# Pooled tokens' block sums at other steps and in another order, and the last pooling product copied to SBUF before its gate

## The chip, the cores and the metric

The kernel runs on one core of a Trainium2 chip. The metric is the device time of one execution in microseconds. The engines are TensorE (PE, matmuls), VectorE (DVE), ScalarE (ACT), GpSimd (POOL) and SyncE (SP, which here only issues DMAs). Each works through its own instructions in order and waits for others by semaphores.

## The reference

One encoder layer, float32, 1024 tokens of width 1024:

```python
h = rmsnorm(x, g_mix)
z = h @ w_in                               # pooled 512 | q 1024 | k 1024 | v 1024
y_pool = pool_mixer(z[..., :512], w_pool_grp, pool_scale)
y_attn = diff_attention(q, k, v, ...)      # 8 heads, two softmax maps per head
gates = sigmoid(h @ w_gate + b_gate)       # 2 x 1024 columns
merged = gates[..., :1024] * (y_pool @ w_branch_pool) \
       + gates[..., 1024:] * (y_attn @ w_branch_attn)
x = x + merged @ w_out
h2 = rmsnorm(x, g_ffn)
x = x + square(relu(h2 @ w_up)) @ w_down
```

The change touches how `y_pool @ w_branch_pool` and its gating are carried out.

## The kernel before, in words

Float32 precision is kept by splitting each operand into a high part (a cast to fp32r on ACT, L137) and a low part (the rest, a subtraction on DVE or POOL, L138). Each product is then three matmuls: high by high (L144), high by low (L145) and low by high (L146). A weight is loaded raw by DMA, cast, and subtracted, before PE may use it; its raw tile is free again after the subtraction. There are two raw tiles in a pool named `raw`.

The kernel has two large parts. In the first, up to about 700 us, a loop over steps `g` (from -2 up to some 10 past the 64 attention steps) builds the projection z of each head (weights `wqkv`, raw `rqkv`), the scores, the softmax and the attention's sums; the gate products `g` (weights `fwgate`, raw `frgate`) and other weight preparation are spread over the steps by tables of step numbers. Then come the two branch projections, each as a Strassen-like scheme of seven products in place of eight: block sums of weights and tokens are made ahead, then products "1", "2", "6", "5", "7", "3", "4" in this order go to PSUM banks named X, Y, Z in turn (pX, pY, pZ for the pooling branch; bX, bY, bZ for the attention branch), and their sums are gated. After this come the output projection and the MLP.

The Tile framework's scheduler sets the final order of the instructions on every engine, from the order of the code, the tiles' dependences and its own timeline. So a change of a step number moves instructions on several engines.

The block sums of the pooling branch are made by `pool_item` (L993). An item (n, e, c) loads a [128, 4, 256] tile by two DMAs (L1004), yields, makes four additions or subtractions of 128x256 on POOL (`sub` is L383, `add` L380), and stores the tile by one DMA to `pw_sum` (weights, n = "w") or `py_sum` (tokens, n = "y") at L1021. The index e picks a depth pair (rows e and e + 2 of the source's four blocks) and c a half of the columns. The "w" items take raw tiles at steps 9, 13, 17 and 21 (`PW_AT`); the "y" items take one of two single tiles, tagged "fu" and "mx", at the steps of `PY_AT`, and read `p_dram`, which holds the pooled tokens. The same two tiles are used by other work: "fu" and "mx" hold weight pieces earlier, the mixer's tiles, the tiles yr2 and yb2 of `y_pair` (L388, attention rows and their factors, L400 and L404), and later the gates `gp`. A load into such a tile waits until the last use of what was in it. In the loop (L1056 to L1063) an item is begun at its step, and its second half, the POOL work and the store, runs one step later.

The pooling products are `p_product` calls from L1243 on. Of the last one, "4", each of four results stays in its bank X[i] until `gated` (L1233) multiplies it there by its gates: a `gp` tile loaded from `g_dram` (L1164) and put through a sigmoid on ACT (L1165); the multiply is L1236, on DVE, into the half-rows `mp` in SBUF. The first attention product then needs the same banks, from the pool `pb` of five: it uses weights `wa` (raw `ra`) and tokens `by`.

Of the kernel before, what the change touches and what calls it, by code (L numbers as in the profile page):

```python
# [17 lines left out]
P = 128  # L18
# [31 lines left out]
G_FIRST, G_Z = 9, 13  # L50
F_FROM, F_PACE, F_UNITS = 4, 0.5, 34
PW_AT = [9, 13, 17, 21]
PY_AT = {63: 'fu', 64: 'mx', 66: 'fu', 67: 'mx'}
SUM_AT = [39, 47, 49, 51, 53, 55, 59, 61]
DIG_AT = {6: 'fu', 8: 'mx', 10: 'fu', 12: 'mx', 14: 'fu', 16: 'mx', 18: 'fu', 20: 'mx'}
DIG_AT.update({g: 'r' for g in (11, 15, 19, 23, 31, 33, 35, 37)})
# [13 lines left out]
def encoder_kernel(  # L70
# [21 lines left out]
    nc = tc.nc  # L92
# [36 lines left out]
    def raw(shape, name):  # L129
        return rpool.tile(shape, F32, tag="raw", name=name)  # L130
# [4 lines left out]
    def split(hi, lo, src, lo_eng=None):  # L135

        made = nc.scalar.copy(hi, src)  # L137
        (lo_eng or nc.vector).tensor_tensor(lo, src, f(hi), op=ALU.subtract)  # L138
        return made
# [17 lines left out]
    def w_tile(shape, name, i, dt=F32R):  # L157
        return wpool.tile(shape, dt, tag=f"W{int(i)}", name=name, bufs=N_W // 2)
# [220 lines left out]
    def add(eng, out_, a, b):  # L379
        eng.tensor_tensor(out_, a, b, op=ALU.add)  # L380

    def sub(eng, out_, a, b):
        eng.tensor_tensor(out_, a, b, op=ALU.subtract)  # L383
# [41 lines left out]
    with ExitStack() as ph:  # L425
# [12 lines left out]
        @contextmanager  # L438
        def behind():
            with ExitStack() as stack:  # L440
                for ins in queued.values():
                    stack.enter_context(tc.issue_after(ins))
                yield
# [17 lines left out]
        def load_x(t):  # L461
            xs[t] = htile([P, D], F32, f"x{t}", 1) if t < 2 else ut([P, D], F32, f"x{t}")
            for c in range(0, D, 512 if t < 2 else D):
                e = c + 512 if t < 2 else D
                loads[f"x{t}"] = q(nc.sync.dma_start, xs[t][:, c:e], x[t * P : (t + 1) * P, c:e])
# [20 lines left out]
        def norm_x(t):  # L486
            if t % 4 == 0:
                hT.update(alloc_T(htile, "hT", t // 4))
            norm_transpose(xs.pop(t), gmb, t, hT, hn_tile(t), sp, [(ps_t, "tr"), (ps_s, "sc")])
# [165 lines left out]
        def distances():  # L655

            di = ut([P, S], I32, "di")
            nc.gpsimd.iota(di, pattern=[[-1, S]], base=S - P, channel_multiplier=1)
            nc.scalar.activation(dist, di, AF.Abs)
            nc.gpsimd.memset(dist[0:64, S - 64 : S], MASKED)  # L660

        def columns():
            cols_ps = ps_t.tile([P, 512], F32, tag="tr", name="cols_ps")
            nc.tensor.transpose(cols_ps[:, 0:32], rows, identf[0:32, 0:32])
            nc.vector.tensor_copy(cols, cols_ps[:, 0:32])
            nc.tensor.transpose(cols_ps[:, P : 2 * P], gg2.rearrange("p a b -> p (a b)"), identf)
            nc.vector.tensor_copy(gcol, cols_ps[:, P : P + 1])
            nc.vector.tensor_scalar(gs, cols[:, 20:21], 1.0 - LAMBDA_INIT, None, op0=ALU.mult)
# [324 lines left out]
        def pool_item(n, e, c, room):  # L993

            name = f"p{n}{e}{c}"
            if room == "r":
                t = raw([P, 4, 256], name)
            else:
                t = fq.tile([P, S], F32, tag=room, name=name).rearrange("p (b c) -> p b c", b=4)
            src, dst = (w_branch_pool, pw_sum) if n == "w" else (p_dram, py_sum)  # L1000
            cs = slice(c * 256, (c + 1) * 256)
            for i in range(2):
                d = e + 2 * i
                nc.sync.dma_start(  # L1004
                    t[:, 2 * i : 2 * i + 2, :],
                    src[d * P : (d + 1) * P, :].rearrange("p (j c) -> p j c", j=2)[:, :, cs],
                )
            yield
            b11, b12, b21, b22 = (t[:, i, :] for i in range(4))
            eng = nc.gpsimd  # L1010
            if n == "w":
                add(eng, b22, b12, b22)
                sub(eng, b12, b11, b12)
                sub(eng, b11, b22, b11)
                sub(eng, b21, b21, b11)
            else:
                sub(eng, b11, b12, b11)
                sub(eng, b12, b22, b12)
                sub(eng, b22, b22, b11)
                sub(eng, b21, b21, b22)  # L1020
            nc.sync.dma_start(dst[:, e, :, cs], t)  # L1021
            yield

        pool_gens = {}
        pool_items = {"w": [(e, c) for c in range(2) for e in range(2)], "y": [(e, c) for c in range(2) for e in range(2)]}
        dig_gens = {}
        sums = [("o", d, c) for d in range(4) for c in range(2)]
        digs = [(e, c) for e in range(4) for c in range(4)]
# [1 line left out]
        for g in range(-2, N + 10):  # L1030
            for t in range(4, NT):
                if LX[t] == g:
                    load_x(t)
            for t in range(1, NT):
                if NX[t] == g:
                    with tc.issue_after(h_hi[t - 2].ins) if t < 6 else nullcontext():
                        norm_x(t)
            if g == G_DIST:
                with behind():
                    distances()  # L1040
            if g == G_COLS:
                columns()
            for a, gen in dig_gens.items():
                if 0 < g - a < 4:
                    next(gen)
            if g in DIG_AT:
                dig_gens[g] = weight_digits(*digs.pop(0), DIG_AT[g])
                with tc.issue_after(loads["x7"].ins), tc.issue_after(loads["fw"].ins):
                    next(dig_gens[g])
            if g in SUM_AT:  # L1050
                sum_gen = weight_sums(*sums.pop(0))
                next(sum_gen)
            if g - 1 in SUM_AT:
                with tc.issue_after(powered[0].ins):
                    next(sum_gen)
            for n, at in (("w", PW_AT), ("y", PY_AT)):  # L1056
                if g - 1 in at:
                    with tc.issue_after(powered[0].ins) if g < N else nullcontext():
                        next(pool_gens[n])
                if g in at:  # L1060
                    pool_gens[n] = pool_item(n, *pool_items[n].pop(0), "r" if n == "w" else PY_AT[g])
                    with tc.issue_after(loads["x7"].ins), tc.issue_after(loads["fw"].ins):
                        next(pool_gens[n])  # L1063
            if g in Y_AT:
                y_gens[g] = y_pair(*Y_AT[g])
                next(y_gens[g])
            for n in (1, 2):
                if g - n in Y_AT:
                    with tc.issue_after(scored[0].ins):
                        next(y_gens[g - n])  # L1070
            gens = {}
            for tok in ORDER:
                if tok not in gens:
                    i = g - tok[1]
                    gens[tok] = stage(tok[0], i) if 0 <= i < N else iter(())
                next(gens[tok], None)
            for gen in gens.values():
                for _ in gen:
                    pass
            while made < F_UNITS and made < (g - F_FROM) * F_PACE:  # L1080
                next(units)
                made += 1
# [34 lines left out]
    def half(d, th):  # L1117
        return mp[d][:, th * 512 : (th + 1) * 512]
# [8 lines left out]
    def p_block(src, i, j):  # L1127
        return src[2 * i * P : (2 * i + 2) * P, j * 512 : (j + 1) * 512].rearrange("(k p) c -> p k c", p=P)

    def wp_set(j):  # L1130
        rw = raw([P, 2, 512], f"rpw{j}")
        with tc.issue_after(loads['fw'].ins) if j in '5734' else nullcontext():
            nc.sync.dma_start(rw, p_block(w_branch_pool, *PW[j]) if j in PW else pw_sum[:, :, PW_SUM[j], :])
        wp_[j] = []
        for k in range(2):
            w = w_tile([P, 2, 512], f"wp{j}_{k}", B_ORDER.index(j) % 2 == 0)
            with tc.issue_after(exped[0].ins) if j in '26' else nullcontext():
                split(w[:, 0], w[:, 1], rw[:, k, :], nc.gpsimd if j in "126" else dve)
            wp_[j].append(w)
# [93 lines left out]
    def gated(d, th, src):  # L1233
        if d % 2 == 0:
            pg[th] = pool_gates(d, th)
        nc.vector.tensor_tensor(half(d, th), src, pg[th][:, d % 2, :], op=ALU.mult)  # L1236
# [4 lines left out]
    X = [pb.tile([P, 512], F32, tag="b", name=f"pX{i}") for i in range(4)]  # L1241
# [37 lines left out]
        gated(i, 1, half(i, 1))  # L1279
    for i in range(4):  # L1280
        p_product(X[i], "4", i)
        gated(i + 4, 0, X[i])
    wa_set("2")
    by_set("2")
    X = [pb.tile([P, 512], F32, tag="b", name=f"bX{i}") for i in range(4)]
# [69 lines left out]
    y = {}  # L1355
# [95 lines left out]
    X = [o_bank(f"oX{t}", t) for t in range(4)]  # L1451
# [453 lines left out]
```

## Time and profile before

| what | value |
| --- | --- |
| median of 3 runs | 1520.74 us (1519.24 to 1521.63) |
| the profiled execution, own time | 1518.36 us |
| its span in the profile | 1516.4 us |
| PE busy | 1503.7 us, 7566 matmuls |
| DVE, ACT, POOL busy | 1076.3, 819.9, 375.2 us |
| DMA moved | 259.39 MB |

Rows of a timeline give the start in us, the duration (of a row with xN, of all N), the engine, the kernel's line, the operation and its tiles as output<-input; a bracket at the end is the idle time before it and what ended it. L12 is line 12 of the kernel. In a table of waits the three numbers are the total, the count and the longest. In a table of windows, each row gives a stretch, its length, the busy time and count of PE, its weight loads, DVE, ACT and POOL, the granted TensorE clock (1.00 is full), the DMA engines' share and GB/s.

### The profile page before, as it was taken

The page shows a single profiled execution, that of the slowest core. Times are in us where ns is not written, and L with a number is a line of the kernel's source. Part 1 is how long each engine was busy: PE and PEld are TensorE (multiplying, and loading weights), DVE is VectorE, ACT ScalarE, POOL GpSimd, SP SyncE. Part 2 cuts the span into 40 slices and gives each one's busy share as a digit, 9 for nine tenths or more (in the row PEclk, how much of TensorE's full clock was granted, in tenths as well). Part 3 has the DMA queues.
Part 4 walks back from the last instruction along what each step waited for, and adds up shares of the span by engine and source line. Part 5 has one row for each costly group of instructions (what it writes and reads, how often), then busy time and mean ns, then how long its engine had stood idle before and what let it go on. Part 6 is the DMA issues. An engine that isn't in the chain of part 4 may idle for free.

```text
span 1516.4 us, 22163 instructions
## 1 busy us (share of the span) xinstructions
PE 1503.7 (99%) x7566; PEld 1303.8 (86%) x7566; DVE 1076.3 (71%) x2196; ACT 819.9 (54%) x1695; POOL 375.2 (25%) x487
## 2 busy tenths in 40 slices
PE   9999999999999999999999999999999999999999
PEld 8999998999999999888788888888888888888887
DVE  7776768887888777745669899676656687556672
ACT  7656565655556564645554478466555634333331
POOL 4556654353526453630240010000000000000000
PEclk9999999999999999999999999999999999999999
DMA  7234443422434344559976734454433799437750
GB/s 228 74 112 144 133 126 105 127 85 70 144 117 146 98 140 142 175 161 295 330 268 204 236 132 136 156 195 153 153 126 111 284 350 392 160 125 261 226 193 28
DMA packets 221931, 259.39 MB, mean 171 GB/s; under 512 B 13462, under 2 KB 152699, under 8 KB 221819
## 3 DMA queue, kind: packets, MB, share of 16 engines
q1 hardware_dynamic: 204250, 230.55, 46.1%
q10 hardware_dynamic: 17568, 27.44, 5.0%
q8 instruction: 59, 0.97, 0.3%
q14 instruction: 54, 0.43, 0.1%
HBM read 180.31 MB, written 77.63 MB: 170 GB/s over the span
## 4 chain that ended last, share of the span: by engine, by line
PE 92%; DMA 4%; POOL 1%; DVE 1%; ACT 1%; issue 1%; SPq 0%; DVEq 0%; POOLq 0%
PE z L146 6%; PE z L144 6%; PE z L145 6%; PE Da L145 4%; PE Da L146 4%; PE Da L144 4%; PE g L146 4%; PE g L144 4%; PE g L145 3%; PE X L144 3%; PE X L146 3%; PE Db L145 3%; PE Db L146 3%; PE X L145 3%; PE Db L144 3%; PE sc L787 2%
## 5 line engine op out<-in xcount | busy, mean ns | idle before, releaser
L146 PE MATMUL z<-wqkv,hT 128*128 128x384 f32 x512 | 174.0, 340 | 0.3 <-DVE hT L449 0.3
L144 PE MATMUL z<-wqkv,hT 128*128 128x384 f32 x512 | 173.6, 340 | 0.1
L145 PE MATMUL z<-wqkv,hT 128*128 128x384 f32 x512 | 172.9, 338 | 0.0
L798 ACT ACTIVATE s<-s,nm 128x256 f32<-128x256 f32 (+7 forms) x128 | 99.4, 777 | 79.4 <-DVE nm L790 79.1
L720 POOL TENSOR_TENSOR ms<-ms,mhalf 128x4 f32<-128x4 f32 x64 | 71.0, 1110 | 155.4 <-DVE ms L719 147.3
L146 PE MATMUL g<-hT,fwgate 128*128 128x512 f32 x256 | 100.9, 396 | 2.7 <-POOL fwgate L138 2.7
L144 PE MATMUL g<-hT,fwgate 128*128 128x512 f32 x256 | 102.0, 398 | 0.3 <-ACT go L353 0.2
L145 PE MATMUL g<-hT,fwgate 128*128 128x512 f32 x256 | 101.3, 396 | 0.0
L144 PEld LDWEIGHTS z<-wqkv,hT 128*128 128x128 f32 x512 | 96.3, 188 | 2.8 <-ACT hT L449 0.4
L145 PEld LDWEIGHTS z<-wqkv,hT 128*128 128x128 f32 x512 | 96.3, 188 | 2.5 <-DVE wqkv L449 0.3
L146 PEld LDWEIGHTS z<-wqkv,hT 128*128 128x128 f32 x512 | 96.2, 188 | 2.6 <-DVE hT L449 0.8
L790 DVE CUSTOM_DVE_ANT_0 s<-sc,dist 128x512 f32<-128x512 f32 (+3 forms) x128 | 71.8, 568 | 19.4 <-PE sc L788 13.9
L138 DVE TENSOR_TENSOR AS<-s,AS 128x512 fp32r<-128x512 f32 x64 | 43.5, 688 | 34.5 <-ACT AS L137 34.3
L787 PE MATMUL sc<-K,Q 128*128 128x512 f32 (+2 forms) x192 | 66.5, 351 | 0.2 <-DVE nm L790 0.2
L788 PE MATMUL sc<-K,Q 128*128 128x512 f32 (+2 forms) x192 | 65.0, 344 | 0.0
L138 POOL TENSOR_TENSOR wqkv<-rqkv,wqkv 128x384 fp32r<-128x384 f32 x56 | 58.8, 1068 | 21.1 <-ACT wqkv L137 21.0
L146 PEld LDWEIGHTS g<-hT,fwgate 128*128 128x128 f32 x256 | 48.5, 189 | 12.4 <-POOL fwgate L138 3.1
L144 PEld LDWEIGHTS g<-hT,fwgate 128*128 128x128 f32 x256 | 48.4, 189 | 9.1 <-ACT yps L344 0.5
L145 PEld LDWEIGHTS g<-hT,fwgate 128*128 128x128 f32 x256 | 48.5, 190 | 8.6 <-issue 0.2
L138 DVE TENSOR_TENSOR AT_0l<-ta,AT_0h 128x512 fp32r<-128x512 f32 (+1 forms) x48 | 32.0, 666 | 29.9 <-ACT AT_0h L137 26.1
L383 POOL TENSOR_TENSOR wd<-wd 128x128 f32<-128x128 f32 (+1 forms) x64 | 49.8, 783 | 8.2 <-ACT wd L985 5.6
L138 POOL TENSOR_TENSOR fwgate<-frgate,fwgate 128x512 fp32r<-128x512 f32 x32 | 42.5, 1333 | 37.0 <-ACT fwgate L137 36.8
(536 smaller groups left out, 4658.2 us busy)
## 6 DMA issues: line engine op xcount, KB each, us to landing
wd<-in_w_down_dram SPq DMA_DIRECT2D x48, 512.0 KB, 6.4
wu<-in_w_up_dram SPq DMA_DIRECT2D x32, 512.0 KB, 5.0
udS<-us SPq DMA_DIRECT2D x64, 256.0 KB, 3.9
ur<-udS SPq DMA_DIRECT2D x32, 512.0 KB, 4.0
rqkv<-in_w_in_dram SPq DMA_DIRECT2D x64, 192.0 KB, 3.0
ur<-ud SPq DMA_DIRECT2D x24, 512.0 KB, 4.0
frgate<-in_w_gate_dram SPq DMA_DIRECT2D x32, 256.0 KB, 2.6
g_dram<-go ACTq DMA_DIRECT2D x32, 256.0 KB, 2.3
```

What stands on the lines that cost most here:

```text
L138: (lo_eng or nc.vector).tensor_tensor(lo, src, f(hi), op=ALU.subtract)
L144: nc.tensor.matmul(ps, lhs_hi, rhs_hi, start=first, stop=False, **kw)
L145: nc.tensor.matmul(ps, lhs_hi, rhs_lo, start=False, stop=False, **kw)
L146: return nc.tensor.matmul(ps, lhs_lo, rhs_hi, start=False, stop=last, **kw)
L383: eng.tensor_tensor(out_, a, b, op=ALU.subtract)
L720: powered[0] = nc.gpsimd.tensor_tensor(ms, ms, mhalf[:, 0:4], op=ALU.pow)
L787: nc.tensor.matmul(dst, Q[:, i, 0, :], rhs, start=True, stop=False)
L788: nc.tensor.matmul(dst, Q[:, i, 1, :], rhs, start=False, stop=True)
L790: nc.vector.tensor_tensor_reduce(out=s[i][:, c : c + w], in0=sc[:, 0:w], in1=dist[:, o0 + c : o0 + c + w], scale=2.0 ** -(h + 1), scalar=B ...
L798: exped[0] = nc.scalar.activation(s[i][:, 0:n], s[i][:, 0:n], AF.Exp, bias=last, scale=-1.0, accum_out=Z[:, i, t : t + 1])
```

## The change

Four edits, and one of spelling.

The "y" items begin at steps 50, 52, 63 and 64; before, at 63, 64, 66 and 67. They are taken by depth pair, both column halves of e = 0 first, then both of e = 1; before, both e of the first column half came first.

The second half of an item runs two steps after its load; before, one. For that the generators are kept under (n, step), since two may be open at a time. This holds for the "w" items too.

The last pooling product is copied by ACT from its bank to its half-row `mp`, and the gating multiply reads and writes that half-row.

```diff
-PY_AT = {63: 'fu', 64: 'mx', 66: 'fu', 67: 'mx'}
+PY_AT = {50: 'fu', 52: 'mx', 63: 'fu', 64: 'mx'}
...
-        pool_items = {"w": [(e, c) for c in range(2) for e in range(2)], "y": [(e, c) for c in range(2) for e in range(2)]}
+        pool_items = {"w": [(e, c) for c in range(2) for e in range(2)], "y": [(e, c) for e in range(2) for c in range(2)]}
...
             for n, at in (("w", PW_AT), ("y", PY_AT)):
-                if g - 1 in at:
+                if g - 2 in at:
                     with tc.issue_after(powered[0].ins) if g < N else nullcontext():
-                        next(pool_gens[n])
+                        next(pool_gens[n, g - 2])
                 if g in at:
-                    pool_gens[n] = pool_item(n, *pool_items[n].pop(0), "r" if n == "w" else PY_AT[g])
+                    pool_gens[n, g] = pool_item(n, *pool_items[n].pop(0), "r" if n == "w" else PY_AT[g])
                     with tc.issue_after(loads["x7"].ins), tc.issue_after(loads["fw"].ins):
-                        next(pool_gens[n])
+                        next(pool_gens[n, g])
...
     for i in range(4):
         p_product(X[i], "4", i)
-        gated(i + 4, 0, X[i])
+        nc.scalar.copy(half(i + 4, 0), X[i])
+        gated(i + 4, 0, half(i + 4, 0))
```

In the compiled order, the four item loads of the changed kernel read the tiles py00, py01, py10 and py11 in this order; before, py00, py10, py01 and py11.

More of the change, by code (lines that the diff above doesn't have):

```diff
@@ L1130, in wp_set @@
     def wp_set(j):
-        rw = raw([P, 2, 512], f"rpw{j}")
+        rw = raw([P, 2, 512], f'rpw{j}')
         with tc.issue_after(loads['fw'].ins) if j in '5734' else nullcontext():
```

## The prediction

> **What bounds the kernel now.** I read the page's busy times first, then its chain, then TensorE's waits, and last the stretches around the two largest of these.
>
> ```profile
> span 1516.4 us, 22163 instructions
> PE 1503.7 (99%) x7566; PEld 1303.8 (86%) x7566; DVE 1076.3 (71%) x2196; ACT 819.9 (54%) x1695; POOL 375.2 (25%) x487
> PE 92%; DMA 4%; POOL 1%; DVE 1%; ACT 1%; issue 1%; SPq 0%; DVEq 0%; POOLq 0%
> ```
>
> TensorE (PE) is busy for 99% of the span and is 92% of the chain. The change takes no matmul away, so all that it can win is time in which PE waits or runs at a lower clock. The view of PE's waits lists these, longest first (microseconds in total, times, longest):
>
> ```profile
> PE g L146 <- POOL fwgate L138: 2.7, 1, 2.7
> ...
> PE bY L144 <- ACT wa L137: 0.9, 1, 0.9
> ...
> PE bX L144 <- DVE mp L380: 0.8, 1, 0.8
> PE bX L146 <- POOL wa L138: 0.6, 1, 0.6
> ```
>
> One wait stands out, a gate product for a weight's low part; the next ones, save two, are in the attention branch's products bX and bY. Both places have windows of their own. The columns after the length are busy time and count for PE, PEld, DVE, ACT and POOL, the granted clock, the DMA share and GB/s:
>
> ```profile
> 641.26:648.69 7.43, 4.71 (x14) 3.36 (x13) 3.92 (x6) 1.95 (x5) 4.13 (x5) 0.77 0.95 299
> 738.86:775.56 36.70, 34.22 (x145) 26.75 (x145) 19.59 (x30) 19.38 (x31) 15.01 (x10) 1.00 0.84 301
> ```
>
> The pitch of an undisturbed 128x512 product is read where bX ends and bZ begins; the first and the last row are five products apart, so 1.13 / 5 = 0.227 us:
>
> ```profile
> 774.43 0.39 PE L145 MATMUL bX<-by,wa 128*128 128x512 f32 x1
> ...
> 775.56 0.39 PE L144 MATMUL bZ<-by,wa 128*128 128x512 f32 x1
> ```
>
> **Stall A, 641 to 649 us.** PE's timeline, then POOL's, with ACT's cast of the weight (the number in brackets is the wait before the row):
>
> ```profile
> 641.26 0.39 PE L145 MATMUL g<-hT,fwgate 128*128 128x512 f32 x1
> 644.36 0.55 PE L146 MATMUL g<-hT,fwgate 128*128 128x512 f32 x1 [2.72 <-POOL fwgate L138]
> 645.13 0.63 PE L145 MATMUL g<-hT,fwgate 128*128 128x512 f32 x1
> 645.56 0.63 PE L146 MATMUL g<-hT,fwgate 128*128 128x512 f32 x1
> 648.69 0.39 PE L144 MATMUL g<-hT,fwgate 128*128 128x512 f32 x1
> ```
> ```profile
> 636.75 0.60 ACT L137 CAST fwgate<-frgate 128x512 fp32r<-128x512 f32 x1
> ```
> ```profile
> 635.60 0.74 POOL L383 TENSOR_TENSOR py<-py 128x256 f32<-128x256 f32 x1 [6.29 <-DMA py<-p_dram]
> ...
> 640.04 3.05 POOL L383 TENSOR_TENSOR py<-py 128x256 f32<-128x256 f32 x4
> 643.05 2.50 POOL L138 TENSOR_TENSOR fwgate<-frgate,fwgate 128x512 fp32r<-128x512 f32 x2
> ```
>
> The cast was done at 637.35, but POOL works in order, and the eight `py` subtractions of two pooled items hold it until 643.05. PE issues nothing from 641.26 to 644.36; then its pitch is 645.56 - 645.13 = 0.43 us until 648.69. The window holds 14 matmuls, 13 of them 128x512: 13 x 0.227 and some 0.07 for the 128x128 one is 3.0 us of work, so the stall costs 7.43 - 3.0 = **4.4 us**, 2.9 as a gap and 1.5 as a lower clock (0.77 granted over the window).
>
> A rule of the Trainium skill bears on that split: "TensorE: Matmul & The Clock Gate", Part 1 (The HAM clock gate), lets the clock fall after an idle window of about 3.4 us. By it a gap this long would not lower the clock and A would be worth 2.9; the rows show a lowered clock after 2.72 us of idling, and the measurement decides.
>
> **Stall B, 738 to 776 us.** The last pooling product's four banks (pX) are read by the gating multiply straight from PSUM, and that waits for the gates (`gp`, a load and a sigmoid). PE's timeline, then DVE's and ACT's:
>
> ```profile
> 738.63 0.39 PE L146 MATMUL pX<-py,wp 128*128 128x512 f32 x1
> 739.80 0.47 PE L144 MATMUL bX<-by,wa 128*128 128x512 f32 x1 [0.78 <-DVE mp L380]
> 742.70 0.50 PE L146 MATMUL bX<-by,wa 128*128 128x512 f32 x1 [0.63 <-POOL wa L138]
> 751.11 0.50 PE L144 MATMUL bY<-by,wa 128*128 128x512 f32 x1 [0.88 <-ACT wa L137]
> 752.98 0.50 PE L146 MATMUL bY<-by,wa 128*128 128x512 f32 x1 [0.19 <-POOL wa L138]
> ```
> ```profile
> 750.48 1.29 DVE L1236 TENSOR_TENSOR mp<-mp,gp 128x512 f32<-128x512 f32 x2 [2.44 <-ACT gp L1165]
> 754.29 1.29 DVE L1236 TENSOR_TENSOR mp<-pX,gp 128x512 f32<-128x512 f32 x2 [2.52 <-ACT gp L1165]
> 756.82 0.69 DVE L1236 TENSOR_TENSOR mp<-pX,gp 128x512 f32<-128x512 f32 x1 [0.54 <-ACT gp L1165]
> ```
> ```profile
> 740.66 1.14 ACT L137 CAST wa<-ra 128x512 fp32r<-128x512 f32 x2 [5.12 <-DMA ra<-in_w_branch_attn_dram]
> ...
> 746.61 0.56 ACT L1289 COPY bx<-bX 128x512 f32<-128x512 f32 x1
> ...
> 750.44 1.14 ACT L137 CAST wa<-ra 128x512 fp32r<-128x512 f32 x2
> ```
>
> pX is done at about 738.9 and its banks come free at 754.9 and later. Till then PE has one bank for bX and is sent on to products whose weights arrive late. From 738.86 to bZ's start at 775.56 there are 144 products (the window counts one more, running in): 144 x 0.227 = 32.7 of 36.70 us, so B costs **4.0 us**.
>
> **The change part by part.** *The items' new steps and the depth pairs.* On POOL, before, around the weight of stall A (fwgate13_0 is that weight; py01 and py11 are the items of steps 66 and 67):
>
> ```order
> L138 TENSOR_TENSOR fwgate12_1_8194<-frgate12_1_8192,fwgate12_1_8194 128x512
> L383 TENSOR_TENSOR py01_7979<-py01_7979 128x256 x3
> L383 TENSOR_TENSOR py11_8028<-py11_8028 128x256
> L830 MEMSET AT7_2_4_7888 128x128 x2
> L383 TENSOR_TENSOR py01_7979<-py01_7979 128x256
> L383 TENSOR_TENSOR py11_8028<-py11_8028 128x256 x3
> L138 TENSOR_TENSOR fwgate13_0_8272<-frgate13_0_8270,fwgate13_0_8272 128x512
> ```
>
> and with the change:
>
> ```order
> L383 TENSOR_TENSOR py11_7820<-py11_7820 128x256
> L138 TENSOR_TENSOR fwgate12_1_8194<-frgate12_1_8192,fwgate12_1_8194 128x512
> L830 MEMSET AT7_2_4_7899 128x128 x2
> L138 TENSOR_TENSOR fwgate13_0_8272<-frgate13_0_8270,fwgate13_0_8272 128x512
> L138 TENSOR_TENSOR fwgate13_1_8277<-frgate13_1_8275,fwgate13_1_8277 128x512
> ```
>
> All eight subtractions have left this place. POOL can start the low part when the cast ends: 637.35 + 1.25 = 638.6. If the MEMSETs wait for their tile as late as before (they stood just ahead of 640.04), it is 640.04 + 1.25 = 641.3, still no later than the slot of 641.49. So A goes whole: **-4.4 us**.
>
> The first two items now run at steps 50 and 52. Each brings four POOL subtractions (3.05 / 4 = 0.76 each, 3.0 an item), a load of two DMAs and a store. On SP, before (yr2_0 is a load of attention rows into the same tile "fu"; rqkv7 are raw weights of the last head):
>
> ```order
> L447 DMA rqkv7_0_6671<-in_w_in_dram 128x3x128 x2
> L278 DMA frgate10_0_7555<-in_w_gate_dram 128x4x128
> L278 DMA frgate10_1_7560<-in_w_gate_dram 128x4x128
> L400 DMA yr2_0_6966<-y_dram_125 128x2x256 x2
> ...
> L447 DMA rqkv7_1_6680<-in_w_in_dram 128x3x128 x2
> L447 DMA rqkv7_2_6689<-in_w_in_dram 128x3x128 x2
> ```
>
> and with the change:
>
> ```order
> L278 DMA frgate10_1_7576<-in_w_gate_dram 128x4x128
> L1004 DMA py00_6171<-p_dram_127 128x2x256 x2
> ...
> L447 DMA rqkv7_1_6696<-in_w_in_dram 128x3x128 x2
> L1021 DMA py_sum_133<-py00_6171 128x4x256
> L400 DMA yr2_0_6982<-y_dram_125 128x2x256 x2
> L447 DMA rqkv7_2_6705<-in_w_in_dram 128x3x128 x2
> ```
>
> So the py00 load takes yr2_0's place, and yr2_0 waits, at the head of SP's queue, until py_sum has landed, with rqkv7_2 and rqkv7_3 behind it. When is that?
>
> ```profile
> 515.42 2.34 SPq L400 DMA_DIRECT2D yr<-y_dram  x2
> ...
> 534.81 4.07 SPq L447 DMA_DIRECT2D rqkv<-in_w_in_dram  x4
> ```
> ```profile
> DMA to landing us min/median/max: 7.4/8.0/8.5
> ```
> ```profile
> 519.85 1.00 POOL L720 TENSOR_TENSOR ms<-ms,mhalf 128x4 f32<-128x4 f32 x1
> ```
>
> The load goes at 515.4, and lands near 518. POOL's subtractions stand around the `ms` row of 519.85 (two ahead, two behind), which goes to about 521.4; the last ends near 523.9. The store lands 7.4 to 8.5 us later (the answer for the py_sum tile), 531.3 to 532.4, so yr2_0's issue and the rqkv7 loads fit ahead of 534.81, where they were released before. Margin 2 us, cost 0; a late landing costs PE about 1 us for each us beyond it. The second item (two steps later) has POOL to itself but for a later `ms`, by 0.8 to 1.8 us, and one DVE wait; I take 0.3, within 0 and 1.
>
> *The second half two steps behind the load.* It also holds for the "w" items of steps 9, 13, 17 and 21, whose raw buffers (two in all) are held a step longer. Head 2's first raw weights were loaded at 121.30, and the first cast of one:
>
> ```profile
> 118.48 0.37 SPq L1021 DMA_DIRECT2D pw_sum<-pw  x1
> ...
> 121.30 0.90 SPq L447 DMA_DIRECT2D rqkv<-in_w_in_dram  x2
> ```
> ```profile
> L137 ACT CAST wqkv<-rqkv x8: 498/513/517, 139.3 to 151.2; 128x384 fp32r<-128x384 f32 x8
> ```
>
> The load moves behind the later store, to 127 or 128 by POOL's order, and still has 11 us. No row shows the new interleaving of steps 9 to 23; the nearest are PE's small waits there, 0.8 the longest, so I allow -1 to +1.5 and take +0.3.
>
> *The copy out of PSUM.* Four more ACT copies of 0.56 us (the row of 746.61), 2.2 us; the DVE multiply from SBUF costs what it did from PSUM (1.29 for two in both rows). What it moves is PE's order. Before, behind pX3 (bX0 is the first bank of attention product 1, with weights wa1; bY is product 2, with wa2; bX0 on by6 is product 6):
>
> ```order
> L146 MATMUL pX3_8521<-py4_1_8805,wp4_1_8797 128x512
> L144 MATMUL bX0_8944<-by1_0_8826,wa1_0_8810 128x512
> ...
> L144 MATMUL bX0_8944<-by1_2_8834,wa1_2_8818 128x512
> ...
> L144 MATMUL bY0_9026<-by2_0_8930,wa2_0_8914 128x512
> ...
> L144 MATMUL bX0_8944<-by6_0_9012,wa6_0_9002 128x512
> ```
>
> and with the change:
>
> ```order
> L146 MATMUL pX3_8521<-py4_1_8805,wp4_1_8797 128x512
> L144 MATMUL bX0_8948<-by1_0_8826,wa1_0_8810 128x512
> ...
> L144 MATMUL bX1_8949<-by1_0_8826,wa1_0_8810 128x512
> ...
> L144 MATMUL bX2_8950<-by1_0_8826,wa1_0_8810 128x512
> L145 MATMUL bX2_8950<-by1_0_8826,wa1_0_8810 128x512
> L144 MATMUL bX0_8948<-by1_2_8834,wa1_2_8818 128x512
> ```
>
> Now 14 products stand ahead of wa1_2's first use in place of 6, and 61 ahead of wa2_2's. With before's arrivals: wa1_2 is wanted at 738.86 + 14 x 0.227 = 742.0, cast at 741.2; wa2_2 at 752.7, cast at 751.0, or 751.6 if a copy stands ahead of it. Margins 0.8 and 1.1, and the copies fit into the 5.12 us that ACT idled before 740.66. B goes: -4.0, of which I keep 0.4 for a cast that slips behind a copy, **-3.6 us**.
>
> The Trainium skill speaks against the copy: "VectorE: DVE Perf Modes", Rules for kernel authors, would copy a matmul's output out of PSUM only for many operations, else read it there. By that rule the sum for this edit would be about 0 or a loss on ACT; the rows show what the rule doesn't weigh, a bank held 16 us.
>
> Sum: -4.4 + 0.3 + 0.3 - 3.6 = -7.4 us. The profiled execution took 1518.36 (span 1516.4), 2.4 below the median of the three runs; the same difference from the median gives 1520.74 - 7.4 = **1513.3**. About 0.2% (3.0 us) is what a measurement of this kernel can tell from no change.
>
> **The rivals.** *The transfers don't move (0.16).* The DMA engines are near full where B lies:
>
> ```profile
> 740.00:750.00 10.00, 9.37 (x39) 6.78 (x38) 1.29 (x2) 4.61 (x7) 5.01 (x4) 1.00 1.04 409
> ```
>
> If ra1_2 lands when it did (its cast at 740.66) while PE comes 4.4 us earlier, PE reaches wa1_2 at 742.0 - 4.4 = 737.6 and waits 3.6 for it, perhaps with the lower clock behind that (1.5). Gain 7.4 - 3.6 = 3.8, or 2.3: 1517 to 1518.4. For it: the share of 1.04; against it: these loads wait for raw buffers that PE's own progress frees.
>
> *Only one stall goes (0.12).* The copies or a sigmoid delay the wa casts, or another weight takes fwgate13_0's place: gain 3.5 to 4.5, 1516 to 1517.
>
> *The edit at 50 and 52 does nothing there (0.04).* Its loads wait for tiles "fu" and "mx", so they may go late enough to be back at stall A: gain from B alone, 1517.
>
> *Slower (0.08): the w items.* With one of two raw buffers held a step longer, each of the four items could make the raw weights queued behind it late for PE. It decides against the change from (7.4 + 3.0) / 4 = 2.6 us an item; at 3.5 an item the time is 1520.7 - 7.4 + 14 = 1527. Against it: the 11 us above.
>
> **How the numbers follow.** Forecast 0.60, rivals 0.16, 0.12, 0.04 and 0.08. The forecast alone spans 1510.8 (both stalls whole and -1.5 elsewhere) to 1515.5; the rivals on the same side reach 1518.4, so 1510.8 to 1518.6 leaves out the slower rival and some of the tails. Faster by over 0.2%: the forecast, the one-stall case and most of the first rival, 0.79; within 0.2%: 0.13; slower: 0.08.
>
> **What would show it.** PE's waits without fwgate, granted clock 1.00 in the 10 us around 640; ACT copies of L1282 before 746; bX0, bX1 and bX2 in turn, and no wait above 0.3 on wa; bZ's start about 32.7 us after the last pX product. Wrong it is if PE waits on rqkv7 or wqkv near 538 to 545, on wa1_2 by more than 1 us, or on wqkv in the first 260 us.

## The result, and the profile after

The changed kernel took 1509.84 us (median of 4 runs, 1507.52 to 1511.16), the kernel before beside it 1519.99 (4 runs): ratio 0.993, 95% interval 0.9913 to 0.9947, so about 8 us faster at the least. The forecast had the direction and the two stalls; the time lies 1 us below its range.

The two profiled executions are closer together than the medians: 1518.36 before, 1511.16 after, 7.2 us, against a forecast of 7.4. Single executions of either kernel differ by several us, and this is part of what follows. Over all runs of this study the kernel before had a median of 1519.2 in 56 runs (1514.7 to 1523.8) and the changed kernel 1510.0 in 14 (1507.5 to 1513.3): **9.2 us** between them.

The page of the changed kernel, first lines:

```profile
span 1508.9 us, 22161 instructions
PE 1500.9 (99%) x7566; PEld 1302.6 (86%) x7566; DVE 1076.1 (71%) x2196; ACT 820.7 (54%) x1699; POOL 372.0 (25%) x487
```

The matmuls are the same in number, and ACT has the four copies more. PE's waits in the changed kernel (total, count, longest):

```profile
PE pX L144 <- ACT mp L1244: 1.3, 2, 0.7
PE warm L449 <- POOL inv L217: 1.1, 1, 1.1
PE X L144 <- ACT U L1651: 0.4, 1, 0.4
PE z L146 <- DVE hT L449: 0.3, 1, 0.3
PE bX L144 <- DVE mp L380: 0.3, 1, 0.3
```

The wait for fwgate, 2.7 us before, is gone, and so are the three waits of bX and bY above 0.5 us. New are two waits of the pooling products for ACT's copies.

Stall A's place now. The windows' columns are as in the forecast; then POOL around the weight:

```profile
630.00:640.00 10.00, 10.00 (x56) 8.61 (x55) 7.07 (x23) 6.71 (x16) 1.29 (x1) 1.00 0.73 221
640.00:650.00 10.00, 10.00 (x50) 8.35 (x49) 4.19 (x12) 3.92 (x9) 1.50 (x2) 1.00 0.18 58
```
```profile
636.79 1.29 POOL L138 TENSOR_TENSOR fwgate<-frgate,fwgate 128x512 fp32r<-128x512 f32 x1 [8.36 <-ACT fwgate L137]
640.87 1.29 POOL L138 TENSOR_TENSOR fwgate<-frgate,fwgate 128x512 fp32r<-128x512 f32 x1 [2.78 <-ACT fwgate L137]
```

PE is busy throughout at a full clock, and POOL, with nothing else to do, subtracts as soon as ACT has cast. Stall B's place, PE's timeline at the start of bX, and the answer for the bZ tile for its first product:

```profile
734.90 0.39 PE L144 MATMUL bX<-by,wa 128*128 128x512 f32 x1
...
736.68 0.50 PE L144 MATMUL bX<-by,wa 128*128 128x512 f32 x1 [0.26 <-DVE mp L380]
```
```profile
L144 PE MATMUL bZ<-by,wa x32: 389/389/389, 768.1 to 800.1; 128*128 128x512 f32 x32
```

From 734.90 to 768.1 are 33.2 us for 144 products, whose bare work is 32.7: 0.5 us lost where 4.0 were.

The load and the store that stand ahead of the last head's raw weights on SP:

```profile
514.25 1.24 SPq L1004 DMA_DIRECT2D py<-p_dram  x2
...
523.10 0.37 SPq L1021 DMA_DIRECT2D py_sum<-py  x1
527.50 1.23 SPq L400 DMA_DIRECT2D yr<-y_dram  x2
533.64 2.86 SPq L447 DMA_DIRECT2D rqkv<-in_w_in_dram  x4
```

yr2_0's load did wait for the store, but only to 527.50; the store landed in 4.4 us (the answer for the py_sum tile), not 7.4 to 8.5, and the weights' loads went at 533.64, a us earlier than before. The margin was 6 us, not 2.

### The profile page after: what moved, and what is told of

Its sections match the earlier page's. It is cut to its first block, busy times and chain, and to the rows that moved or that the text cites. A ratio compares the mean times of both kernels' runs of the same rounds, so it can differ in the third digit from the quotient of the medians.

```text
span 1508.9 us, 22161 instructions
## 1 busy us (share of the span) xinstructions
PE 1500.9 (99%) x7566; PEld 1302.6 (86%) x7566; DVE 1076.1 (71%) x2196; ACT 820.7 (54%) x1699; POOL 372.0 (25%) x487
## 4 chain that ended last, share of the span: by engine, by line
PE 92%; DVE 3%; DMA 2%; ACT 1%; issue 1%; SPq 0%; DVEq 0%; ACTq 0%
PE z L146 5%; PE z L144 5%; PE z L145 5%; PE Da L145 4%; PE Da L144 4%; PE Da L146 4%; PE g L144 4%; PE g L146 4%; PE g L145 4%; PE X L144 3%; PE X L146 3%; PE Db L145 3%; PE Db L144 3%; PE X L145 3%; PE Db L146 3%; PE sc L787 2%
```

## The experiments

All times are medians; "before" is the kernel before in the same group of runs, on the same chip: 1518.8 (15 runs) for the first three experiments that name it, 1519.5 (9) for the changed kernel's third time, 1519.4 (17) for the others. An interval in brackets is the 95% interval of the ratio, or what it comes to in us.

**The changed kernel again**, without an edit.

> The changed kernel once more, unedited. Theory (the profile of before was an execution with little lost, the profile of after one with much lost): medians 9 to 11 us apart as before, and this execution's profile shows the stalls by the weight fwgate13_0 and after the last pooling product gone, waits of 0 to 1.5 us of the pooling products on ACT's copies. Rival (the first result was a draw of few runs): medians 7 to 8 us apart.

1510.6 against 1518.8, ratio 0.9942 (0.993 to 0.9955). That is 8.2 us, between the range of the theory and that of the rival, so neither is borne out by the time. This execution's profile, of the slowest of the five runs (1513.27), has another wait at the top:

```profile
PE po L881 <- DVE oqs L138: 1.3, 2, 1.2
```

A wait of 1.2 us at 689 us, for an attention block's low part (`oqs`), stands here, and the waits on ACT's copies, 1.3 us in the changed kernel's first profile, are down to 0.2. The stalls A and B are gone in both.

**Without the copy.**

```diff
-        nc.scalar.copy(half(i + 4, 0), X[i])
-        gated(i + 4, 0, half(i + 4, 0))
+        gated(i + 4, 0, X[i])
```

> The changed kernel without the copy of the last pooling product (steps, pair order and two-step delay stay). Theory, the parts add: stall A (4.4) and about 1 us before 275 us go, the waits after the last pooling product stay at 2.5 us or more; time 4.5 to 6 us below before. Rival, the transfers behind the last pooling product don't move with TensorE: the earlier TensorE loses there 2 to 4 us more than before, and the time is only 1 to 3 us below before.

1513.3 against 1518.8, 0.9956 (0.9942 to 0.9969): 5.5 us faster. The rival, at 1 to 3 us, falls. The parts add about: 5.5 here and 3.35 for the copy alone (next) make 8.8 us, against 8.2 for both in the same group of runs. PE's waits hold no fwgate, and the one behind the last pooling product stands at the top:

```profile
PE bX L144 <- DVE mp L380: 2.3, 1, 2.3
PE warm L449 <- POOL inv L217: 1.1, 1, 1.1
```

It is a wait for a bank: without the copies only the one that DVE's `add` on pZ frees is to be had. It was 0.8 us in the first profile of before and 1.6 in the second, but there three more waits, for `wa`, followed it, and all four came to 2.5 and 3.3 us; here it is the only one. So the waits at B are no longer than before in sum. In this execution a lowered clock followed the wait (last section).

**Only the copy**, on the kernel before.

```diff
-        gated(i + 4, 0, X[i])
+        nc.scalar.copy(half(i + 4, 0), X[i])
+        gated(i + 4, 0, half(i + 4, 0))
```

> The kernel before with only the copy of the last pooling product. Theory, the parts add: the wait for fwgate of 2.7 us and its lower clock stay, the waits after the last pooling product go; time 3.5 to 4.5 us below before, and the pooling products don't wait for ACT's copies, since TensorE comes there as late as before. Rival, the wait of the pooling products on ACT's copies (1.3 us in the changed kernel) comes from the copy edit: it shows here too, and the gain is 2 to 2.5.

1515.45 against 1518.8, 0.9975 (0.9963 to 0.9986): 3.35 us, just under the 3.5 to 4.5 expected. The interval (2.1 to 5.6) holds that range, and most of the rival's 2 to 2.5 too, so the time alone does not decide between them. PE's waits keep A and lose B:

```profile
PE g L146 <- POOL fwgate L138: 3.2, 1, 3.2
...
PE bX L144 <- ACT wa L137: 0.2, 1, 0.2
```

The rival's sign, the waits on ACT's copies (L1244), is not there; and the kernel before, run again without any edit (below), does have one such wait, of 0.4 us. So they are no price of the copy edit as such. What A costs in this execution is 3.2 us of waiting, more than in the profile of before.

**The weights' items one step behind their loads**, all else as changed.

```diff
-                if g - 2 in at:
+                late = 1 if n == "w" else 2
+                if g - late in at:
                     with tc.issue_after(powered[0].ins) if g < N else nullcontext():
-                        next(pool_gens[n, g - 2])
+                        next(pool_gens[n, g - late])
```

> The changed kernel with the weights' items (steps 9, 13, 17, 21) back to one step behind their loads; the tokens' items stay at two. Theory, the 1 to 1.2 us that the changed kernel lost less between 225 and 275 us come from the weights' delay: they return, with the waits for DVE at 250 and 252 us, and the time is about 1 us above the changed kernel's. Rival, the delay did nothing there: within 0.4 of the changed kernel, and no such waits.

1511.4 against 1510.6 for the changed kernel beside it. The waits at 250 us are back, as the theory has it; the difference of the medians, 0.8, is in the right direction and too small for this many runs. So the two were run beside each other once more, the changed kernel first:

> The changed kernel a third time, beside the next one. Theory: 8 to 9 us below before; no wait of TensorE above 0.4 us between 225 and 275 us, and none for fwgate.

1509.4 against 1519.5, 0.9934 (0.9921 to 0.9946): 10.1 us, above the expected range. The two signs held: no wait for fwgate, and none above 0.4 us between 225 and 275 us.

> The changed kernel with the weights' items one step behind their loads, a second time, beside the changed kernel. Theory: the waits for DVE at 250 and 252 us are there again (1.2 us in all) and the median is 0.5 to 1.5 us above the changed kernel's of this call. Rival: the waits are there but the executions differ by more than that anyway, and the medians are within 0.4.

1510.6, 1.2 us above the changed kernel, and each of its five executions (1510.5 to 1512.0) lies above each of the changed kernel's five (1508.6 to 1510.4). The view of PE's timeline at the place, of this kernel, rows with a wait:

```profile
250.81 0.63 PE L843 MATMUL ta<-identf,s 128*128 128x128 f32 x4 [0.38 <-DVE s L807]
252.25 0.44 PE L843 MATMUL ta<-identf,s 128*128 128x128 f32 x2 [0.81 <-DVE AT L138]
252.85 0.50 PE L787 MATMUL sc<-K,Q 128*128 128x512 f32 x1 [0.17 <-DVE nm L790]
```

and of the changed kernel beside it:

```profile
252.75 0.33 PE L146 MATMUL z<-wqkv,hT 128*128 128x384 f32 x1
252.93 0.34 PE L144 MATMUL z<-wqkv,hT 128*128 128x384 f32 x1
253.10 0.60 PE L843 MATMUL ta<-identf,s 128*128 128x128 f32 x4
253.46 0.42 PE L145 MATMUL z<-wqkv,hT 128*128 128x384 f32 x1
253.72 0.34 PE L146 MATMUL z<-wqkv,hT 128*128 128x384 f32 x1
```

In the kernels with the delay the head's projection (z) is still under way here, with 37 or more of its products to come between 249 and 262 us, and they fill the time in which DVE works on the scores and on yr; in those without it 10 or 11 are left there, and PE waits 0.38 + 0.81 + 0.17 = 1.4 us. All six profiles without the delay (before twice, copy only, new steps only, and this edit twice) show the waits for `s` and `AT` at this place. All six with it (the changed kernel three times, without the copy, the casts behind the copies, the old steps) do not; they have one wait of 0.2 us near 256 us instead. PE's idle time between 225 and 275 us is 1.3 to 1.4 us in the former and 0.2 in the latter, so the delay of the weights' items gains 1.1 us there, which the medians' 0.8 and 1.2 fit. Why the scheduler places the projection later for it was not tried.

**The casts of the first attention tokens behind the copies.** The changed kernel's first profile has this on ACT, where the cast of `by` waits and the copies (L1244) that free the banks stand behind it:

```profile
700.52 0.59 ACT L1244 COPY mp<-pX 128x512 f32<-128x512 f32 x1 [0.53 <-PE pX L146]
707.63 1.14 ACT L137 CAST by<-ry 128x512 fp32r<-128x512 f32 x2 [6.51 <-DMA ga<-g_dram]
708.67 0.58 ACT L1244 COPY mp<-pX 128x512 f32<-128x512 f32 x1
```

```diff
-        nc.scalar.copy(half(i, 0), X[i])
+        copied = [nc.scalar.copy(half(i, 0), X[i])]
...
-                split(t[:, 0, :], t[:, 1, :], rw[:, k, :])
+                with tc.issue_after(copied[0].ins) if j == "1" else nullcontext():
+                    split(t[:, 0, :], t[:, 1, :], rw[:, k, :])
```

(The first line stands behind `p_product(X[i], "1", i)`, the others in `by_set`.)

> The changed kernel with the casts of the first attention tokens (by1) put behind the fourth copy of pooling product 1 on ACT. Theory: ACT stood waiting for by1's rows with two of those copies queued behind it, and TensorE waited for the copies (1.3 us in one execution, 0.2 in the other); that wait goes, and the time is 0.5 to 1.5 us below the changed kernel's. Rival, TensorE then waits as long for the weights of bX or for by1: within 0.4 of the changed kernel, with the wait at 735 to 745 us.

1511.5 against 1519.4, 0.9942 (0.993 to 0.9954): 8.0 us, no better than the changed kernel's 8.2 and 10.1. The wait is gone from its profile, and the one at the start of bX too, with nothing in their place there. The two longest waits that are left both lie in the first 30 us:

```profile
PE warm L449 <- POOL inv L217: 1.1, 1, 1.1
PE z L144 <- ACT hT L449: 0.7, 1, 0.7
```

Yet the changed kernel's third profile has no such wait either, unedited. The expected gain failed: the copies were late in one execution by 1.3 us, in another by 0.2 and in a third by nothing, so there is little on average to win. Whether the edit wins 0.3 us can't be told from 6 runs.

**The tokens' items at the old steps**, all else as changed.

```diff
-PY_AT = {50: 'fu', 52: 'mx', 63: 'fu', 64: 'mx'}
+PY_AT = {63: 'fu', 64: 'mx', 66: 'fu', 67: 'mx'}
```

> The changed kernel with the tokens' items back at steps 63, 64, 66 and 67 (pair order, two-step delay and copy stay). Theory, stall A comes from eight subtractions beside fwgate13_0 and goes only with the steps: the wait for fwgate of 2.5 to 3.5 us is back with its lower clock; time 4 to 5 us above the changed kernel's. Rival, the two-step delay alone keeps POOL from waiting on the items' loads: that wait is under 1 us, and the time is within 1.5 us of the changed kernel's.

1513.8 against 1519.4, 0.9957 (0.9946 to 0.9969). That is 3.8 us above the changed kernel's median of all runs, slightly under the 4 to 5 expected (the changed kernel was not run in this group: against before the gain is 5.6 us here, and was 8.2 and 10.1 for the changed kernel). The wait is back:

```profile
PE g L146 <- POOL fwgate L138: 2.6, 1, 2.6
```

The delay alone does not clear A; the step numbers do.

**Only the new steps and the pair order**, on the kernel before.

```diff
-PY_AT = {63: 'fu', 64: 'mx', 66: 'fu', 67: 'mx'}
+PY_AT = {50: 'fu', 52: 'mx', 63: 'fu', 64: 'mx'}
...
-"y": [(e, c) for c in range(2) for e in range(2)]
+"y": [(e, c) for e in range(2) for c in range(2)]
```

> The kernel before with only the new steps and the pair order; the second halves stay one step behind, and no copy. Theory: stall A goes, all else stays; 3.5 to 5 us below before. Rival, with one step POOL and SP wait for the loads and the store of steps 50 and 52, and rqkv7 behind them: waits for wqkv of 1 us or more at 535 to 545 us, and a gain of under 2.5.

1514.3 against 1519.4, 0.9958 (0.9946 to 0.997): 5.1 us (4.6 to 8.2 by the interval), at the upper end or above it. PE waits neither for fwgate nor for wqkv. So for the tokens' items the two-step delay is not needed to clear A. B stands as before or larger:

```profile
PE bX L144 <- DVE mp L380: 1.5, 1, 1.5
...
PE bX L144 <- ACT wa L137: 0.7, 1, 0.7
PE bX L146 <- POOL wa L138: 0.6, 1, 0.6
```

The new steps with the old pair order were not tried: the item of step 52 would then read the depth pair whose last pooled tokens are written too late. In the changed kernel's profile the last write of `p_dram` was issued at 542.03 us, the load of step 52 at 537.68.

**The kernel before again**, without an edit.

> The kernel before once more, unedited. Theory on why executions of one kernel differ by up to 7 us: the same waits on transfers come out longer or shorter; this profile shows the waits for fwgate (2.5 to 3.5) and behind the last pooling product (2 to 4 in all) again, and its span differs from 1516.4 by what all of TensorE's waits differ. Rival, a lower clock somewhere: equal waits, and windows with a granted clock under 0.95 apart from that at 645 us.

1518.4 (11 runs) against 1519.4 (17), 0.9992 (0.9981 to 1.0003): the same kernel, as it should be. The profiled execution's span is 1518.2, 1.8 above the first profile's. Its waits:

```profile
PE g L146 <- POOL fwgate L138: 2.6, 1, 2.6
PE bX L144 <- DVE mp L380: 1.6, 1, 1.6
PE ta L843 <- DVE AT L138: 1.5, 2, 0.8
...
PE bY L144 <- ACT wa L137: 0.8, 1, 0.8
PE bX L146 <- POOL wa L138: 0.6, 1, 0.6
```

A and B are there; the wait for the bank is 0.8 us longer than in the first profile, and a second wait for AT adds 0.7. The matmuls of both executions are the same, in the same order, so their starts can be set side by side. This execution lost 0.4 us in the first 100 us, 1.3 more by 500 us (most of it around the second wait for AT, at 413), 0.8 by 600, and 1.1 between 700 and 800; and it won 1.8 back at stall A, where its clock stayed full. That makes the 1.8 us between them. So longer waits, as the theory has it, and the clock, as the rival has it, both had a part, with opposite signs; no window here has a granted clock under 0.95.

## Why the prediction was right or wrong

**Stall A, -4.4: right, and 0.2 us short.** It goes, for the reason given: with only the old steps back the wait of 2.6 us is there, and with only the new steps it is gone. The forecast's sum counted one product too many: of the window's 14 matmuls one was running in, as it says of the window of B, so the work was 12 x 0.227 + 0.07 = 2.8 us and A cost 4.6 us, 2.9 as a gap and 1.7 as a lower clock. By that the sum would have been -7.6 and the time 1513.1. Nor is its size one number. PE's wait was 2.6 to 3.2 us in four executions, and the lower clock behind it came in three of the four; so A cost from 2.8 us (before again, with no lower clock) to 5.1 (the window of the copy alone, below: 7.80 less 2.7 of work), and the new steps alone gained 5.1.

**The rivals of A did not occur.** The first two items do move to where the table says, loaded at 514.25 and 537.68 rather than near 635, and no weight took fwgate13_0's place.

**The queue at rqkv7, 0: right**, by a bound that was too careful: 4.4 us for the store's landing, not 7.4 to 8.5. The forecast's last subtraction was late by a us as well: its own rows give 521.4 + 2 x 0.76 = 522.9, not 523.9, and in the trace it ended at 522.7. The 0.3 for the second item is not to be seen.

**The weights' items, +0.3 within -1 to +1.5: the step that failed.** I had costed the delay by where it could hold up raw weights, and took the middle of the bounds with a small loss. The rows were there to ask the other way: three small waits of PE, 1.4 us in all, at 250 us, in the stretch whose order the delay changes. In the profile of before they are these:

```profile
250.60 0.63 PE L843 MATMUL ta<-identf,s 128*128 128x128 f32 x4 [0.37 <-DVE s L807]
252.04 0.44 PE L843 MATMUL ta<-identf,s 128*128 128x128 f32 x2 [0.81 <-DVE AT L138]
252.64 0.50 PE L787 MATMUL sc<-K,Q 128*128 128x512 f32 x1 [0.17 <-DVE nm L790]
```

The forecast named the longest of them as a measure of its uncertainty, and not as time to be won. The delay gained 1.1 us there, so the term had the wrong sign and lay at the lower end of its bounds. The slower rival, built on the same edit, had its sign wrong too.

**The copy, -3.6: right in mechanism and about right in size.** The order on PE is as forecast, B's loss fell from 4.0 to 0.5 in the profiles, and the copy alone gained 3.35. The margin for wa1_2, 0.8 us in the forecast, was overstated:

```profile
737.73 1.14 ACT L137 CAST wa<-ra 128x512 fp32r<-128x512 f32 x2 [4.16 <-DMA ra<-in_w_branch_attn_dram]
```

The first cast of the pair ended at 738.3 and the 15th product of bX, which needs it, started at 738.63. So 0.3 us was left.

**The transfers don't move: partly.** The first and last start of the pX products, before and after, by the answers for that tile:

```profile
L144 PE MATMUL pX<-py,wp x32: 389/389/497, 703.3 to 738.2; 128*128 128x512 f32 x32
```
```profile
L144 PE MATMUL pX<-py,wp x32: 389/389/497, 697.6 to 734.2; 128*128 128x512 f32 x32
```

PE came 5.7 us earlier to the first pooling product but 4.0 earlier to the last, and the wa1_2 cast moved by 2.9 (740.66 to 737.73). The lag was paid in that execution as 1.3 us of waits on ACT's copies; in the third profile of the changed kernel there is none. In the kernel without the copy the wait for the bank is longer (2.3 us, against 0.8 and 1.6 in the profiles of before), but the waits for `wa` that followed it are gone.

**The base: the other term that was off.** The gain was taken off a median of three runs, 1520.74; the median of 56 is 1519.2. Of the 3.5 us between 1513.3 and 1509.84, 1.5 is the base, 1.4 the weights' items (+0.3 taken, about -1.1 measured), 0.3 the second item and 0.2 the size of A; the little that is left means nothing beside the spread of four runs. From 1519.2 the same range would start at 1509.3 and hold the result, so the base alone put it outside. With runs this wide, a range whose lower end is the sum of both stalls from the median of three was too narrow. And that the two profiled executions differ by 7.2 us, so near the forecast's 7.4, is luck: the medians differ by 9.2. In the chances, the 0.79 for faster takes in 0.07 of the first rival's 0.16, which is less than the "most" of it that is named there.

## What to carry to other kernels

When an engine that works in order holds up the busiest one, look for what stands ahead of the late instruction and move that, not the late instruction. A matmul's result waiting in PSUM for something unrelated (here a gate) holds a bank that the next product wants: a copy on an idle engine can pay though it makes no operation cheaper. And when an edit reorders a stretch, cost it by the small waits that are there now as well as by those it could make.

## What the runs showed of the hardware

A gap of PE of two to three us may lower its clock or not. Four windows that begin with or just ahead of such a gap (granted clock is the third number from the end): before again with a wait of 2.56 us, the kernel without the copy with 2.29, the old steps with 2.61, and only the copy with 3.2:

```profile
644.00:651.00 7.00, 4.43 (x20) 3.50 (x20) 3.58 (x6) 1.69 (x4) 3.81 (x4) 1.00 0.99 315
```
```profile
733.67:742.00 8.33, 6.04 (x20) 4.69 (x20) 3.06 (x5) 3.43 (x5) 5.01 (x4) 0.80 1.04 410
```
```profile
641.50:648.00 6.50, 3.89 (x13) 2.98 (x13) 3.64 (x6) 1.72 (x4) 3.88 (x4) 0.83 0.97 313
```
```profile
642.20:650.00 7.80, 4.60 (x14) 3.46 (x14) 3.07 (x6) 1.80 (x5) 5.16 (x5) 0.78 0.84 264
```

A gap of 2.29 us lowered the clock and one of 2.56 did not. None of the shorter ones behind the first 10 us did in any of the 12 profiles; the longest of these was 1.61 us. Where the clock was lowered, it was 0.50 for 3.41 us each time (before from 644.67, copy only from 645.98, old steps from 645.75, without the copy from 736.68), whatever the gap had been. That costs a PE with work at hand up to 3.41 x 0.50 = 1.7 us. The pitch is then 0.43 us in place of 0.227, and in the old steps' execution the lowered stretch began 1.5 us after the gap's end:

```profile
644.26 0.50 PE L146 MATMUL g<-hT,fwgate 128*128 128x512 f32 x1 [2.61 <-POOL fwgate L138]
...
645.53 0.41 PE L145 MATMUL g<-hT,fwgate 128*128 128x512 f32 x1
645.75 0.61 PE L146 MATMUL g<-hT,fwgate 128*128 128x512 f32 x1
646.17 0.63 PE L144 MATMUL g<-hT,fwgate 128*128 128x512 f32 x1
```

Each execution's mean granted clock shows how often it happens. It was below 1.000 in 41 of the 52 executions of the kernel before for which it was kept, in 7 of 10 with only the copy and in 3 of 6 with the old steps, the three kernels that have stall A; and in 3 of 40 of the five kernels without A. The 41 have a median of 1519.5 us, the other 11 of 1516.6. So part of what the new steps win is this clock (1.7 of the 4.6 us in the profile of before), and part of the spread between executions of the kernel before goes with it. Why the two groups lie 2.9 us apart, and not 1.7, is not shown.

So the length of the gap does not decide alone, and no run here shows what does. The Trainium skill, "TensorE: Matmul & The Clock Gate", Part 1 (The HAM clock gate), says that the window in which activity is judged runs freely, and by that the outcome would depend on where in it a gap falls; the five gaps (these four, and the 2.72 us of the forecast) agree with this, but not with a gap of about 3.4 us as the least that costs clock. For a forecast on these runs, a gap of 2.3 to 3.2 us is worth its own length plus up to 1.7 us.
